# One-tile ring slots: weight and attention tiles merged into 8 KB tiles, and a ring of 23 slots instead of 21

## The chip, the cores and the metric

The kernel runs on one core of a Trainium2 chip. The core has five engines that run side by side, each with its own order of instructions: TensorE (PE; its weight loads are shown as PEld), VectorE (DVE), ScalarE (ACT), GpSimd (POOL) and SyncE (SP). Data come from the chip's large memory by DMA; here every transfer is issued by SP, in order, and carried by 16 DMA engines. The metric is the time of one execution on the device, in microseconds (us).

## What is computed

The reference is a pair of transformer blocks on 256 tokens of width 1024, in float32, followed by a norm. The first block has stick-breaking and latent attention, a feed-forward of width 2816 with a convolution of width 3, and a gate on an embedding per layer. The second has modulated norms, a convolution module, an attention over the selected keys, a pool mixer, an output projection, and a mixture of 32 experts of which each token takes two:

```python
def reference(x, ...):
    x = first_block(x, p, positions, ...)
    return second_block(x, c_2, mod_w_2, ...)

def second_block(x, c, ...):                       # one layer
    mod = silu(c) @ mod_w + mod_b                  # sh1, sc1, g1, sh2, sc2, g2
    h = rmsnorm(x, norm1_g) * (1 + sc1) + sh1
    a_val, a_gate, cq, ckv, qi, ki, wi, u_pool = split(h @ w_in)
    mix = concat([conv_module(a_val, a_gate),      # depthwise, width 31
                  dsa_attention(cq, ckv, qi, ki, wi),
                  pool_mixer(u_pool)]) @ w_out
    x = x + g1 * mix
    h = rmsnorm(x, norm2_g) * (1 + sc2) + sh2
    x = x + g2 * hier_moe(h, ..., w1, w3, w2)      # 32 experts, top 2
    return rmsnorm(x, final_g)
# an expert: (silu(h @ w1[e]) * (h @ w3[e])) @ w2[e], 1024 -> 512 -> 1024
```

The weights of one expert are 3 x 1024 x 512 float32, 6.3 MB, and all 32 are read: 201 MB of the 300 MB that the kernel moves.

## The kernel before

The work follows the reference in time. The first block and the first part of the second (to about 455 us) are matrix products whose float32 weights are cut into a high and a low part; each product is three matmuls (`mm3`, L265 to L269). A weight arrives as a raw tile of 8 KB per partition (pool `wr`, tag `raw`, three buffers), and `split` (L271) makes the two parts from it: `wh` by a cast on ScalarE and `wl` by a subtraction on VectorE (L283), each in a tile of 4 KB per partition.

The experts are the last stage (the loop at the end of the program). Expert e first multiplies the gathered tokens by w1 and w3 (`eu`, L1659), then by w2 (`ey`, L1686). Its weights come as six pieces of 1 MB, [128 x 2048] float32, 8 KB in each of 128 partitions; pieces 0 to 3 of an expert are w1 and w3, 4 and 5 are w2. Piece i is in slot i modulo the length of a ring of slots. The ring grows while the second block runs: `grow` (L1128) adds a slot and loads the next piece into it. The places of the slots are those of tiles that the program doesn't need any more, so that a load waits until their last reader is done. The 21 slots, in the order of the list `ring`, which is the order of the pieces:

- 0 to 3: pool `ewa` (step "ea" in ORDER); 4 and 5: two operands of the first block ("eh", "el"); 6: a raw tile ("e1");
- 7: the tiles qT and k2T of the second block's attention ("e2"); 8: lnT and v2 ("e3"); 9 and 10: two es tiles each ("e4"); of these pairs each tile holds half of a piece, in 4 KB per partition;
- 11 and 12: raw tiles; 13 and 14: pairs of wh and wl ("es"); 15 and 16: two operands; 17 and 18: pairs of wh and wl; 19 and 20: pool `ewc`, with room only after the router's work is closed.

`load_piece` (L1097) issues one transfer of 1 MB for a slot of one tile, and two of 512 KB for a pair; piece i is a DMA whose destination is named ew and the number of the piece, and for a pair with a further digit 0 or 1 (ew70 and ew71 are the halves of piece 7, ew11 is all of piece 11). The last three pieces are cut finer: 189 in two halves, 190 and 191 in eight of 256 KB (`exp_last`). In the expert loop six pieces are loaded behind each expert's `ey`. The tiles `fin` and `fg` of the final norm (L1639) take two slots of the ring near the end.

PE's order is written by hand, for the second block in the string ORDER (L50), whose steps are functions. The order on the other engines is made by a scheduler from the program's dependences; SP's too. SP issues in this order, so that a transfer that waits for its slot holds all behind it. The tiles are placed in pools, on two sides of the memory; `N_MP` is the number of tiles for weights of the modulation (r_mod) that are loaded ahead during the feed-forward (`F_ahead`), into a place on the right side that the second block's tiles take later.

Some names that the prediction uses: r_cq, r_ckv, r_qi, r_cv, r_wu, r_up and r_out are raw weight tiles of the second block; w_lt the parts of r_cq and r_ckv; gq, nrow, pw, rw and rb small operands; y_n the normed input, res_ple the first block's last summand; cb a sum of the width-31 convolution on POOL (L1255), s_a the pool mixer's running sums there (L1278 to L1288); ppt_d the transposes of the attention's weights (L778), pgs those of the gate matrix (L1655).

Of the kernel before, what the change touches and what calls it, by code (L numbers as in the profile page):

```python
# [20 lines left out]
P = 128  # L21
D = 1024
# [12 lines left out]
CONV2 = 31  # L35
N_A = 4
N_B = 3
N_C = 2
N_TAP = 12
# [5 lines left out]
OUT_G = ()  # L45
N_MP = 6
MOE_K = 2
X_AT = {(2, 9): 4, (31, 9): 1, (31, 10): 1}
LAST = 'y01 y12 x2 m02 y24 m24'
ORDER = 'qi0 kT0 qi1 kT1 ix0 ix1 cv0 li0 li1 cv1 ea ea lo0 lo1 ae lw ea ea va0 up eh el qk0 qk1 qk2 qk3 va1 d0 sm0 d1 po sm1 w3 e1 e2 c60 c61 w1 dT0 do0 c70 c71 c20 w2 dT1 c30 do1 tp e3 e4 e4 rl g1 c21 c31 c40 w0 ct e1 e1 c50 c51 c41 es es co'  # L50
W_AT = (2,)
# [13 lines left out]
def block_pair_kernel(ctx, tc, A, out, dbg=None):  # L65
# [205 lines left out]
    def split(raw, name, shape, gain=None, eng=V, first=()):  # L271
        n = math.prod(shape)
        vs = []
        for tg in ("wh", "wl"):
            v = wsp.tile([P, 1024], F32R, tag=tg, name=f"{name}_{tg}")[:, :n]
            if len(shape) == 2:
                v = v.rearrange("p (a b) -> p a b", a=shape[0])
            elif len(shape) == 3:
                v = v.rearrange("p (a b c) -> p a b c", a=shape[0], b=shape[1])
            vs.append(v)  # L280
        if gain is None:
            hi = S.copy(vs[0], raw)
            lo = eng.tensor_tensor(vs[1], raw, vs[0].bitcast(F32), op=ALU.subtract)  # L283
            for i, l in zip((hi, lo), first):
                after(i, *l)
                l[:] = [i]
        else:
            act(vs[0], raw, AF.Copy, scale=gain)
            V.scalar_tensor_tensor(vs[1], raw, gain, vs[0].bitcast(F32), op0=ALU.mult, op1=ALU.subtract)
        return vs  # L290
# [351 lines left out]
    def mla_weights():  # L642
        wqv = raw_pk("w_q_up", 0, (2, 768), "r_wqup")
        wqn, wqr = [[wsp.tile([P, 1024], F32R, tag=t_, name=f"{nm}_{t_}")[:, :2 * n].rearrange("p (k n) -> p k n", k=2)
                     for t_ in ("wh", "wl")] for nm, n in (("wqn", 512), ("wqr", 256))]
        for k in range(2):
            src = wqv[:, k, :].rearrange("p (h d) -> p h d", d=96)
            hv, lv = [t[:, k, :].rearrange("p (h d) -> p h d", d=64) for t in wqn]
            S.copy(hv, src[:, :, 0:64])
            V.tensor_sub(lv, src[:, :, 0:64], hv.bitcast(F32))  # L650
            for r in range(2):
                s3 = src[:, r::2, 64:96]
                hv, lv = [t[:, k, :].rearrange("p (c r d) -> p c r d", r=2, d=ROPE)[:, :, 1 - r, :] for t in wqr]
# [441 lines left out]
    etiles, ring, last = {}, [], []  # L1095

    def load_piece(i):  # L1097

        e, kind = divmod(i, 6)
        p_, tag, shape = ring[i % len(ring)]  # L1100
        if i >= 6 * N_EXP - 2:

            assert tag == "ew"
            v = p_.tile(shape, F32, tag=tag, name=f"ew{i}").rearrange("p (j k n) -> p j k n", j=4, k=2)
            last.append((v, kind - 4))
# [5 lines left out]
            return  # L1111
        if isinstance(tag, tuple):
            ts = [p_.tile([P, 1024], F32, tag=tg, name=f"ew{i}{k}") for k, tg in enumerate(tag)]
            for k, t_ in enumerate(ts):
                load(t_, packed("exp", i, 1024, 1024 * k))
        else:
            t_ = p_.tile(shape, F32, tag=tag, name=f"ew{i}")
            if len(shape) == 3:
                t_ = t_.rearrange("p k n -> p (k n)")
            ts = [t_[:, 1024 * k:1024 * k + 1024] for k in range(2)]  # L1120
            if i < 6 * N_EXP - 3:
                load(t_, packed("exp", i, 2048))
            else:
                for k in range(2):
                    load(ts[k], packed("exp", i, 1024, 1024 * k))
        form = "p (m n) -> p m n" if kind < 4 else "p (j n) -> p j n"
# [11 lines left out]
    bp = pool("b2", 1, mt, side="right")  # L1138
    esp = pool("b2e", 4, mt, side="right")
    m2 = pool("m2", 1, mt, side="right")  # L1140
    def tmp2(name):
        return esp.tile([P, D], F32, tag="es", name=name)

# [5 lines left out]

    lnT = bp.tile([P, 4, SEQ], F32, tag="lnT", name="lnT")[:, 0:3]  # L1150
    wi = bp.tile([P, NB, 8], F32, name="wi")
    qiT = bp.tile([P, 4, SEQ], F32, tag="qT", name="qiT")
    kiT = bp.tile([P, SEQ], F32, tag="ki", name="kiT")
# [22 lines left out]
    def ln_in(b):  # L1176
# [3 lines left out]
        if not lns:  # L1180
            lns[-1] = tmp2("ln2").rearrange("p (b n) -> p b n", b=2)
        ln = lns[b] = lns[-1][:, b, 0:384]
# [123 lines left out]

    k2T = bp.tile([P, 4, SEQ], F32, tag="k2T", name="k2T")
    v2 = halves(bp.tile([P, D], F32, tag="v2", name="v2"))
    lw, q2 = [], []

    def lat_load():
        q2.append(bp.tile([P, 4, SEQ], F32, tag="qT", name="q2T"))
        wu = raw_pk("w_lat2", 0, (4, 512), "r_wu")
        lw.extend(wu[:, 2 * i:2 * i + 2] for i in range(2))
# [19 lines left out]
    def dsa_softmax(b):  # L1334
        es2[b] = es_tiles(b, f"es2{b}", tmp2)
        softmax(lg2[b], b, 64.0 ** -0.5, selb[b], es2[b], f"d{b}")

    def dsa_T(b):
        pts2[b] = [tmp2(f"PT2{b}{kb}").rearrange("p (h q) -> p h q", h=8) for kb in range(b + 1)]
        att_T(es2[b], b, pts2[b], f"d{b}")  # L1340
# [57 lines left out]
    def router_load():  # L1398
# [9 lines left out]
             "ae": lambda: act_set("exp_and_others", SET_LATE[1]),  # L1408
             "e1": lambda: grow(wr, 1, "raw"), "es": lambda: grow(wsp, 1, ("wh", "wl")),
             "e2": lambda: grow(bp, 1, ("qT", "k2T")), "e3": lambda: grow(bp, 1, ("lnT", "v2")),  # L1410
             "e4": lambda: grow(esp, 1, ("es", "es")), "g1": lambda: M2.update(g1=mod_bc2("g1", 1, 0))}
    for i in range(4):
# [142 lines left out]
    grow(ap_, 1, "al", (P, KC, SEQ))  # L1555
    grow(wsp, 2, ("wh", "wl"))
    grow(ewc, N_C)

# [49 lines left out]
    for e in range(N_EXP):  # L1608
# [261 lines left out]
```

## Time and profile before

| | |
|---|---|
| median of 3 runs | 966.21 us (964.25 to 966.93) |
| the profiled execution | 965.9 us, its span 964.1 us |
| PE busy | 796.6 us (83%) |
| DVE, ACT, POOL busy | 450.4 (47%), 322.1 (33%), 96.3 us (10%) |
| moved by DMA | 301.24 MB, 312 GB/s over the span |

The profile is of one execution. The span runs from the first to the last instruction that it shows, and 1.8 us of the execution's time lie around it. Busy shares are means over stages with different limits, so that the stages are read apart, by windows of the time axis. "Idle before" is the time that an engine stood still ahead of a group of instructions, with what ended most of it. The queue of SP shows when a transfer was issued and what its issue waited for.

### The profile page before, as it was taken

How to read it: one execution, taken by the hardware profiler on the slowest of the kernel's cores; microseconds unless marked ns; L12 is line 12 of the kernel's file. 1: busy time of each engine (PE TensorE's matmuls, PEld its weight loads, DVE VectorE, ACT ScalarE, POOL GpSimd, SP SyncE). 2: the span in 40 equal slices, each digit the busy share in tenths (PEclk: the TensorE clock that was granted, in tenths of full speed). 3: DMA queues.
4: the chain of work that ended last, by engine and by line, in shares of the span. 5: the costliest groups of instructions: out<-in, count | busy, mean ns of one | idle time of the engine just before them, and what ended most of it. 6: DMA issues, size and time to landing. Idle time of an engine off the chain costs nothing. (4 is left out here: it accounts for less than half of the span.)

```text
span 964.1 us, 17534 instructions
## 1 busy us (share of the span) xinstructions
PE 796.6 (83%) x7228; PEld 571.5 (59%) x7228; DVE 450.4 (47%) x992; ACT 322.1 (33%) x635; POOL 96.3 (10%) x178
## 2 busy tenths in 40 slices
PE   5999989999999996996988987676677676756874
PEld 5978759999999873984675644233343242422422
DVE  5656667766766767589863322112121121211213
ACT  5637755555555665456741000000000000000100
POOL 1321310000000115107010000000000000000000
PEclk9999999999999998898898999879797897897978
DMA  7857788865454545855289999999999999999994
GB/s 267 274 220 271 267 343 317 306 217 177 171 193 162 188 161 162 329 223 197 80 340 372 413 421 415 418 418 416 421 414 422 414 422 415 419 416 418 418 414 168
DMA packets 55975, 301.24 MB, mean 312 GB/s; under 512 B 6480, under 2 KB 7508, under 8 KB 30292
## 3 DMA queue, kind: packets, MB, share of 16 engines
q1 hardware_dynamic: 55892, 300.08, 79.7%
q8 instruction: 58, 0.95, 0.4%
q14 instruction: 25, 0.20, 0.1%
HBM read 299.01 MB, written 1.05 MB: 311 GB/s over the span
## 5 line engine op out<-in xcount | busy, mean ns | idle before, releaser
L1659 PE MATMUL eu<-ew,XT 128*32 128x256 f32 x2048 | 144.9, 409 | 58.5 <-DMA ew<-in_exp_dram 58.2
L1659 PEld LDWEIGHTS eu<-ew,XT 128*32 128x32 f32 x2048 | 58.9, 114 | 134.3 <-DMA ew<-in_exp_dram 74.9
L77 ACT ACTIVATE hm<-eu 128x128 f32<-128x128 f32 x32 | 8.9, 277 | 340.5 <-PE eu L1659 340.5
L1686 PE MATMUL ey<-ew,hmT 128*32 128x256 f32 (+2 forms) x1088 | 85.0, 449 | 33.5 <-DMA ew<-in_exp_dram 22.5
L1672 DVE TENSOR_TENSOR hm<-hm,eu 128x128 f32<-128x128 f32 x32 | 9.2, 287 | 153.2 <-ACT hm L77 153.2
L1686 PEld LDWEIGHTS ey<-ew,hmT 128*32 128x32 f32 x1088 | 33.2, 125 | 73.0 <-DMA ew<-in_exp_dram 35.1
L1697 DVE TENSOR_TENSOR eys<-ey,g2y 128x256 f32<-128x256 f32 x31 | 13.2, 425 | 108.3 <-PE ey L1686 108.3
L269 PE MATMUL u<-hF_h,w_g_wl 128*128 128x256 f32 x168 | 47.6, 283 | 0.0
L267 PE MATMUL u<-hF_h,w_g_wh 128*128 128x256 f32 x168 | 47.5, 283 | 0.0
L268 PE MATMUL u<-hF_l,w_g_wh 128*128 128x256 f32 x168 | 47.5, 283 | 0.0
L216 POOL TENSOR_SCALAR ep_fin<-msf 128x2 f32<-128x2 f32 x1 | 0.2, 236 | 456.8 <-DVE msf L1776 456.8
L268 PE MATMUL u<-hF_l,w_v_wh 128*128 128x256 f32 x160 | 45.3, 283 | 0.0
L269 PE MATMUL u<-hF_h,w_v_wl 128*128 128x256 f32 x160 | 45.3, 283 | 0.0
L267 PE MATMUL u<-hF_h,w_v_wh 128*128 128x256 f32 x160 | 45.2, 283 | 0.0
L1588 PE MATMUL moe<-eys,gT 32*128 32x256 f32 (+1 forms) x528 | 41.8, 430 | 1.4 <-DVE eys L1710 1.4
L1622 PEld LDWEIGHTS px<-hr,x 128*128 128x128 f32 x256 | 35.1, 223 | 5.5 <-issue 2.4
L283 DVE TENSOR_TENSOR w_dn_wl<-r_d,w_dn_wh 128x1024 fp32r<-128x1024 f32 x22 | 27.0, 1225 | 24.4 <-ACT w_dn_wh L77 24.4
L77 ACT ACTIVATE XT<-px,c_SH,c_G 128x128 f32<-128x128 f32 x32 | 14.6, 457 | 69.8 <-DVE XT L1630 69.8
L1669 DVE COPY gT<-pgs 128x256 f32<-128x256 f32 x32 | 13.6, 424 | 51.6 <-PE pgs L1655 51.4
L1622 PE MATMUL px<-hr,x 128*128 128x128 f32 x256 | 36.9, 310 | 0.7 <-DVE hr L1614 0.7
L283 DVE TENSOR_TENSOR w_v_wl<-r_gv,w_v_wh 128x1024 fp32r<-128x1024 f32 x22 | 30.2, 1372 | 12.0 <-ACT w_v_wh L77 12.0
L269 PE MATMUL dn<-w_dn_wh,acl 128*128 128x512 f32 x88 | 34.5, 393 | 0.1
(568 smaller groups left out, 1961.2 us busy)
## 6 DMA issues: line engine op xcount, KB each, us to landing
ew<-in_exp_dram SPq DMA_DIRECT2D x117, 1024.0 KB, 15.3
ew<-in_exp_dram SPq DMA_DIRECT2D x146, 512.0 KB, 12.6
r_mod<-in_mod_w_dram SPq DMA_DIRECT2D x24, 1024.0 KB, 7.8
r_gv<-in_w_up_dram SPq DMA_DIRECT2D x22, 1024.0 KB, 4.9
r_d<-in_w_down_dram SPq DMA_DIRECT2D x11, 1024.0 KB, 4.9
r_wo<-in_w_o_dram SPq DMA_DIRECT2D x4, 1024.0 KB
r_pg<-in_w_ple_gate_dram SPq DMA_DIRECT2D x4, 1024.0 KB, 4.8
r_out<-in_w_out_dram SPq DMA_DIRECT2D x4, 1024.0 KB
```

Source lines behind the costliest of these rows:

```text
L77: i = getattr(nc.scalar, name)(*a, **kw)
L267: T.matmul(o, l[0], r[0], start=start, stop=False, skip_group_check=True)
L268: T.matmul(o, l[0], r[1], start=False, stop=False, skip_group_check=True)
L269: T.matmul(o, l[1], r[0], start=False, stop=stop, skip_group_check=True)
L283: lo = eng.tensor_tensor(vs[1], raw, vs[0].bitcast(F32), op=ALU.subtract)
L1588: T.matmul(moe[c][:, b * 256:b * 256 + 256][:, js], gT[rs, TB[b]], yt[rs, js], start=(start and b == 0), stop=stop, skip_group_check=True)
L1622: T.matmul(pt[:, j * P:(j + 1) * P], x[b][:, k * P:(k + 1) * P], hr[:, b], start=(b == 0), stop=(b == 1))
L1659: T.matmul(u[32 * g_:32 * g_ + 32, 0:2 * P], XT[:, k, 32 * i:32 * i + 32], etiles[6 * e + k // 2][k % 2][:, :, P * g_:P * g_ + P], start=( ...
L1669: V.tensor_copy(gT, pg[:, :SEQ])
L1672: V.tensor_mul(hm, hm, u[:, P:2 * P])
L1686: T.matmul(y[32 * c:32 * c + 32, 0:64 * (js.stop - js.start)], hmT[:, 32 * k:32 * k + 32], w2e[k].rearrange("p j (c i) -> p c j i", c=4)[: ...
L1697: V.tensor_mul(yt, y[:, 0:256], g2y)
```

## The change

The pairs of 4 KB tiles become single tiles of 8 KB: `split` makes one tile `w` whose halves are the high and the low part; lnT and v2 are the halves of `lv`, qiT (later q2T, in its place) and k2T those of `qk`; four es tiles become two double ones. Each slot of the ring is then one tile, and each piece but the last three is one transfer. The ring gets two slots more, one in `ewa` and one in `ewc`, and two more r_mod tiles are loaded ahead in the feed-forward. The scratch for DMA descriptors, 16 KB per partition by default, is set to 1 KB; this gives the room.

```diff
@@ -33 +33 @@
-N_A = 4
+N_A = 5
 N_B = 3
-N_C = 2
+N_C = 3
...
-N_MP = 6
+N_MP = 8
...
-ORDER = 'qi0 kT0 qi1 kT1 ix0 ix1 cv0 li0 li1 cv1 ea ea lo0 lo1 ae lw ea ea va0 up eh el qk0 qk1 qk2 qk3 va1 d0 sm0 d1 po sm1 w3 e1 e2 c60 c61 w1 dT0 do0 c70 c71 c20 w2 dT1 c30 do1 tp e3 e4 e4 rl g1 c21 c31 c40 w0 ct e1 e1 c50 c51 c41 es es co'
+ORDER = 'qi0 kT0 qi1 kT1 ix0 ix1 cv0 li0 li1 cv1 ea ea lo0 lo1 ae lw ea ea ea va0 up eh el qk0 qk1 qk2 qk3 va1 d0 sm0 d1 po sm1 w3 e1 e2 c60 c61 w1 dT0 do0 c70 c71 c20 w2 dT1 c30 do1 tp e3 e4 e4 rl g1 c21 c31 c40 w0 ct e1 e1 c50 c51 c41 es es co'
@@ -140 +140 @@
+    def halves2(t):
+        return [t[:, D * i:D * i + D] for i in range(2)]
@@ -271 +274 @@ split
-        for tg in ("wh", "wl"):
-            v = wsp.tile([P, 1024], F32R, tag=tg, name=f"{name}_{tg}")[:, :n]
+        t_ = wsp.tile([P, 2048], F32R, tag="w", name=f"{name}_w")
+        for i in range(2):
+            v = t_[:, 1024 * i:1024 * i + n]
@@ -1094 +1099 @@ load_piece
+    def piece_tile(i):
+        p_, tag, shape = ring[i % len(ring)]
+        t_ = p_.tile(shape, F32, tag=tag, name=f"ew{i}")
+        return t_.rearrange("p k n -> p (k n)") if len(shape) == 3 else t_
...
-        if isinstance(tag, tuple):
-            ts = [p_.tile([P, 1024], F32, tag=tg, name=f"ew{i}{k}") for k, tg in enumerate(tag)]
-            for k, t_ in enumerate(ts):
-                load(t_, packed("exp", i, 1024, 1024 * k))
+        t_ = piece_tile(i)
+        ts = [t_[:, 1024 * k:1024 * k + 1024] for k in range(2)]
+        if i < 6 * N_EXP - 3:
+            load(t_, packed("exp", i, 2048))
         else:
...
@@ -1136 +1137 @@
-    esp = pool("b2e", 4, mt, side="right")
+    esp = pool("b2e", 2, mt, side="right")
...
+    es_t = [halves2(esp.tile([P, 2 * D], F32, tag="es", name=f"es2{i}")) for i in range(2)]
...
-    lnT = bp.tile([P, 4, SEQ], F32, tag="lnT", name="lnT")[:, 0:3]
+    lv, qk_ = [halves2(bp.tile([P, 2 * D], F32, tag=nm, name=nm)) for nm in ("lv", "qk")]
+    lnT = lv[0].rearrange("p (c t) -> p c t", c=4)[:, 0:3]
...
-    qiT = bp.tile([P, 4, SEQ], F32, tag="qT", name="qiT")
+    qiT, k2T = [t.rearrange("p (c t) -> p c t", c=4) for t in qk_]
@@ -1304 +1305 @@
-    k2T = bp.tile([P, 4, SEQ], F32, tag="k2T", name="k2T")
-    v2 = halves(bp.tile([P, D], F32, tag="v2", name="v2"))
-    lw, q2 = [], []
+    v2 = halves(lv[1])
+    lw, q2 = [], [qiT]
@@ -1332 +1331 @@
-        es2[b] = es_tiles(b, f"es2{b}", tmp2)
+        es2[b] = [t.rearrange("p (h k) -> p h k", h=8 // (b + 1)) for t in ([es_t[0][1]], es_t[1])[b]]
...
-        pts2[b] = [tmp2(f"PT2{b}{kb}").rearrange("p (h q) -> p h q", h=8) for kb in range(b + 1)]
+        pts2[b] = [t.rearrange("p (h q) -> p h q", h=8) for t in ([es_t[0][0]], es_t[0])[b]]
@@ -1406 +1405 @@ steps
-             "e1": lambda: grow(wr, 1, "raw"), "es": lambda: grow(wsp, 1, ("wh", "wl")),
-             "e2": lambda: grow(bp, 1, ("qT", "k2T")), "e3": lambda: grow(bp, 1, ("lnT", "v2")),
-             "e4": lambda: grow(esp, 1, ("es", "es")), "g1": lambda: M2.update(g1=mod_bc2("g1", 1, 0))}
+             "e1": lambda: grow(wr, 1, "raw"), "es": lambda: grow(wsp, 1, "w"),
+             "e2": lambda: grow(bp, 1, "qk"), "e3": lambda: grow(bp, 1, "lv"),
+             "e4": lambda: grow(esp, 1, "es"), "g1": lambda: M2.update(g1=mod_bc2("g1", 1, 0))}
@@ -1553 +1552 @@
-    grow(wsp, 2, ("wh", "wl"))
+    grow(wsp, 2, "w")
     grow(ewc, N_C)
@@ -1637 +1636 @@
-            fin = ap_.tile([P, KC, SEQ], F32, tag="ah", name="fin").rearrange("p (b k) t -> p b (k t)", b=2)
-            fg = ap_.tile([P, KC, SEQ], F32, tag="al", name="fg").rearrange("p k t -> p (k t)")[:, 0:D]
+            fin = bp.tile([P, 2 * D], F32, tag="lv", name="fin").rearrange("p (b n) -> p b n", b=2)
+            fg = bp.tile([P, 2 * D], F32, tag="qk", name="fg")[:, 0:D]
@@ -1856 +1855 @@
-    nc = _bacc.Bacc("TRN2", target_bir_lowering=False, num_devices=1)
+    nc = _bacc.Bacc("TRN2", target_bir_lowering=False, num_devices=1, dynamic_dma_scratch_size=1024)
```

SP has 477 instructions before and 405 after. Three places of its order follow; the number behind an underscore only tells buffers apart. The first is the transfers between the first block's end and the second conv weight r_cv1, before:

```order
L139 DMA r_qi1_4341<-in_w_in2_c_dram 128x2048
L139 DMA pw_4264<-in_pool_w_dram 128x128
L139 DMA r_cv0_4524<-in_w_in2_c_dram 128x2048
L139 DMA ew0_4677<-in_exp_dram 128x2048
L139 DMA ew1_4679<-in_exp_dram 128x2048
L139 DMA ew2_4695<-in_exp_dram 128x2048
L139 DMA r_cv1_4616<-in_w_in2_c_dram 128x2048
L139 DMA ew3_4697<-in_exp_dram 128x2048
L139 DMA ew4_4779<-in_exp_dram 128x2048
```

and now:

```order
L139 DMA r_cv0_4413<-in_w_in2_c_dram 128x2048
L139 DMA gq2_4153<-in_q_norm_g_2_dram 128x256
L139 DMA gq2_4153<-in_kv_norm_g_2_dram 128x128
L139 DMA nrow2_4126<-in_norm2_g_2_dram 32x512 x2
L139 DMA ew5_4662<-in_exp_dram 128x2048
L139 DMA ew0_4561<-in_exp_dram 128x2048
L139 DMA pw_4159<-in_pool_w_dram 128x128
L139 DMA ew1_4563<-in_exp_dram 128x2048
L139 DMA ew2_4578<-in_exp_dram 128x2048
L139 DMA ew3_4580<-in_exp_dram 128x2048
L139 DMA ew4_4582<-in_exp_dram 128x2048
L139 DMA r_cv1_4502<-in_w_in2_c_dram 128x2048
```

The conv weights r_cv0 stand ahead of gq2 and nrow2, piece 5 and pieces 0 to 4 (with pw among them) are all ahead of r_cv1; before it was pieces 0 to 2.

The second is the queue around the attention's end, from the last raw weight of the output projection r_out0 on, before (ew70 and the like are half pieces):

```order
L139 DMA r_out0_5184<-in_w_out_2_dram 128x2048
L139 DMA ew70_4923<-in_exp_dram 128x1024
L139 DMA ew71_4924<-in_exp_dram 128x1024
L139 DMA ew90_5146<-in_exp_dram 128x1024
L139 DMA ew91_5147<-in_exp_dram 128x1024
L139 DMA ew81_5143<-in_exp_dram 128x1024
L139 DMA ew100_5150<-in_exp_dram 128x1024
L139 DMA ew101_5151<-in_exp_dram 128x1024
L139 DMA ew11_5221<-in_exp_dram 128x2048
L139 DMA ew12_5223<-in_exp_dram 128x2048
```

and now, with whole pieces, in which ew8 lies in `qk`, ew9 in `lv`, ew10 and ew11 in the es tiles, ew12 and ew13 in raw tiles:

```order
L139 DMA r_out0_5047<-in_w_out_2_dram 128x2048
L139 DMA ew8_4801<-in_exp_dram 128x2048
L139 DMA ew10_5013<-in_exp_dram 128x2048
L139 DMA ew12_5082<-in_exp_dram 128x2048
L139 DMA ew9_5011<-in_exp_dram 128x2048
L139 DMA ew11_5015<-in_exp_dram 128x2048
L139 DMA ew13_5084<-in_exp_dram 128x2048
L139 DMA ew14_5104<-in_exp_dram 128x2048
```

At the place where ew90 and ew91 stood there is ew10, the double tile of the second query block's weights; ew9 comes behind ew12.

The third is the last new slots and the first slots that are used again, before (the ring has 21 slots, ew21 is the first that takes the place of an expert piece):

```order
L139 DMA ew180_5500<-in_exp_dram 128x1024
L139 DMA ew181_5501<-in_exp_dram 128x1024
L139 DMA ew19_5504<-in_exp_dram 128x2048
L139 DMA ew20_5506<-in_exp_dram 128x2048
L139 DMA ew21_5619<-in_exp_dram 128x2048
L139 DMA ew22_5621<-in_exp_dram 128x2048
L139 DMA ew23_5623<-in_exp_dram 128x2048
```

and now (23 slots, the first that takes such a place is ew23):

```order
L139 DMA ew17_5351<-in_exp_dram 128x2048
L139 DMA ew18_5353<-in_exp_dram 128x2048
L139 DMA ew19_5355<-in_exp_dram 128x2048
L139 DMA ew20_5357<-in_exp_dram 128x2048
L139 DMA ew21_5359<-in_exp_dram 128x2048
L139 DMA ew22_5361<-in_exp_dram 128x2048
L139 DMA ew23_5474<-in_exp_dram 128x2048
L139 DMA ew24_5476<-in_exp_dram 128x2048
```

The first reuse moved by two pieces.

## Rows read from the trace of the kernel before

**Rows 1.** The page, GB/s moved in 40 equal slices of the span
```profile
GB/s 267 274 220 271 267 343 317 306 217 177 171 193 162 188 161 162 329 223 197 80 340 372 413 421 415 418 418 416 421 414 422 414 422 415 419 416 418 418 414 168
```

**Rows 2.** Windows: us, engines busy (instructions), PE clock, DMA share, GB/s; expert stage
```profile
600.00:700.00 100.00, 69.03 (x792) 31.83 (x792) 16.19 (x52) 3.49 (x10) 0.00 (x0) 0.85 1.02 418
...
800.00:900.00 100.00, 71.15 (x808) 34.93 (x812) 17.79 (x56) 5.32 (x14) 0.00 (x0) 0.85 1.02 418
```

**Rows 3.** The page's groups: busy us, mean ns, idle before and its releaser
```profile
L1659 PE MATMUL eu<-ew,XT 128*32 128x256 f32 x2048 | 144.9, 409 | 58.5 <-DMA ew<-in_exp_dram 58.2
...
L269 PE MATMUL u<-hF_h,w_g_wl 128*128 128x256 f32 x168 | 47.6, 283 | 0.0
```

**Rows 4.** Waits of SP's queue: waited for, us in total, times, longest
```profile
SPq L139 <- DMA ew<-in_exp_dram: 327.2, 229, 2.7
...
SPq L139 <- PE ppt_d L778: 26.5, 1, 26.5
...
SPq L139 <- PE pgs L1655: 13.7, 7, 10.9
```

**Rows 5.** Windows between the second block's attention and expert 0
```profile
395.00:446.00 51.00, 48.96 (x388) 45.19 (x386) 41.85 (x100) 32.16 (x63) 14.13 (x22) 1.00 0.61 234
...
455.00:475.00 20.00, 17.42 (x81) 11.88 (x78) 18.16 (x52) 15.86 (x44) 0.83 (x1) 0.79 0.02 5
...
475.00:513.00 38.00, 34.82 (x240) 29.36 (x242) 25.02 (x87) 17.68 (x38) 3.53 (x8) 0.91 0.89 338
...
502.00:513.00 11.00, 8.06 (x64) 7.21 (x67) 5.86 (x36) 3.64 (x9) 0.00 (x0) 0.69 1.00 408
...
513.00:514.00 1.00, 1.00 (x18) 0.36 (x10) 1.00 (x5) 0.46 (x1) 0.00 (x0) 1.00 0.45 188
...
516.00:517.00 1.00, 0.83 (x16) 0.26 (x8) 0.11 (x1) 0.10 (x1) 0.00 (x0) 1.00 1.00 393
```

**Rows 6.** Timeline of SP's queue: start, us, issue, count
```profile
473.65 0.33 SPq L139 DMA_DIRECT2D ew<-in_exp_dram  x1
...
513.79 6.79 SPq L139 DMA_DIRECT2D ew<-in_exp_dram  x6
...
934.95 11.16 SPq L139 DMA_DIRECT2D ew<-in_exp_last_dram  x8
```

**Rows 7.** Timeline of PE, idle before in brackets: the pool product, expert 0
```profile
453.97 1.97 PE L1296 MATMUL ppl<-s_a,pw 64*64 64x256 f32 x8 [7.79 <-POOL s_a L1288]
...
512.66 1.07 PE L1659 MATMUL eu<-ew,XT 128*32 128x256 f32 x16
```

**Rows 8.** DMA view, packets of four windows: 621:638, 730:743, 535:543, 642:649
```profile
DMA packets 997, 7.25 MB, mean 426 GB/s; under 512 B 112, under 2 KB 112, under 8 KB 112
...
DMA packets 762, 5.56 MB, mean 428 GB/s; under 512 B 83, under 2 KB 83, under 8 KB 83
...
DMA packets 892, 3.27 MB, mean 409 GB/s; under 512 B 97, under 2 KB 97, under 8 KB 891
...
DMA packets 781, 2.86 MB, mean 408 GB/s; under 512 B 88, under 2 KB 88, under 8 KB 776
```

**Rows 9.** The page's queue and its issues: count, KB each, us to landing
```profile
q1 hardware_dynamic: 55892, 300.08, 79.7%
...
ew<-in_exp_dram SPq DMA_DIRECT2D x117, 1024.0 KB, 15.3
ew<-in_exp_dram SPq DMA_DIRECT2D x146, 512.0 KB, 12.6
```

**Rows 10.** Timeline of POOL: one addition cb
```profile
451.79 0.72 POOL L1255 TENSOR_TENSOR cb<-cb,pr 128x256 f32<-128x256 f32 x1
```

**Rows 11.** Timelines of DVE and SP; instructions on r_cv, first and last start
```profile
384.57 0.68 DVE L1052 TENSOR_TENSOR y_n<-y_n,SH 128x512 f32<-128x512 f32 x1
...
386.37 1.88 DVE L283 TENSOR_TENSOR w_lt_wl<-r_ckv,w_lt_wh 128x800 fp32r<-128x800 f32 x2
...
400.52 0.33 SPq L139 DMA_DIRECT2D r_cv<-in_w_in_c_dram  x1
...
L77 ACT CAST w_cv_wh<-r_cv x4: 1045/1047/1047, 403.3 to 412.0; 128x1024 fp32r<-128x1024 f32 x4
```

More of the change, by code (lines that the diff above doesn't have):

```diff
@@ L643, in mla_weights @@
         wqv = raw_pk("w_q_up", 0, (2, 768), "r_wqup")
-        wqn, wqr = [[wsp.tile([P, 1024], F32R, tag=t_, name=f"{nm}_{t_}")[:, :2 * n].rearrange("p (k n) -> p k n", k=2)
-                     for t_ in ("wh", "wl")] for nm, n in (("wqn", 512), ("wqr", 256))]
+        wqn, wqr = [[t_[:, 1024 * i:1024 * i + 2 * n].rearrange("p (k n) -> p k n", k=2) for i in range(2)]
+                    for t_, n in ((wsp.tile([P, 2048], F32R, tag="w", name="wqn"), 512),
+                                  (wsp.tile([P, 2048], F32R, tag="w", name="wqr"), 256))]
         for k in range(2):
@@ L1095, in block_pair_kernel @@
     etiles, ring, last = {}, [], []
+    def piece_tile(i):
+        p_, tag, shape = ring[i % len(ring)]
+        t_ = p_.tile(shape, F32, tag=tag, name=f"ew{i}")
+        return t_.rearrange("p k n -> p (k n)") if len(shape) == 3 else t_
     def load_piece(i):
         e, kind = divmod(i, 6)
-        p_, tag, shape = ring[i % len(ring)]
         if i >= 6 * N_EXP - 2:
-            assert tag == "ew"
-            v = p_.tile(shape, F32, tag=tag, name=f"ew{i}").rearrange("p (j k n) -> p j k n", j=4, k=2)
+            v = piece_tile(i).rearrange("p (j k n) -> p j k n", j=4, k=2)
             last.append((v, kind - 4))
@@ L1111, in load_piece @@
             return
-        if isinstance(tag, tuple):
-            ts = [p_.tile([P, 1024], F32, tag=tg, name=f"ew{i}{k}") for k, tg in enumerate(tag)]
-            for k, t_ in enumerate(ts):
-                load(t_, packed("exp", i, 1024, 1024 * k))
-        else:
[L1117 to L1125, printed above, removed]
+        t_ = piece_tile(i)
+        ts = [t_[:, 1024 * k:1024 * k + 1024] for k in range(2)]
+        if i < 6 * N_EXP - 3:
+            load(t_, packed("exp", i, 2048))
+        else:
+            for k in range(2):
+                load(ts[k], packed("exp", i, 1024, 1024 * k))
         form = "p (m n) -> p m n" if kind < 4 else "p (j n) -> p j n"
@@ L1138, in block_pair_kernel @@
     bp = pool("b2", 1, mt, side="right")
-    esp = pool("b2e", 4, mt, side="right")
+    esp = pool("b2e", 2, mt, side="right")
     m2 = pool("m2", 1, mt, side="right")
-    def tmp2(name):
-        return esp.tile([P, D], F32, tag="es", name=name)
+    es_t = [halves2(esp.tile([P, 2 * D], F32, tag="es", name=f"es2{i}")) for i in range(2)]
     def w1k(name):
@@ L1180, in ln_in @@
         if not lns:
-            lns[-1] = tmp2("ln2").rearrange("p (b n) -> p b n", b=2)
+            lns[-1] = es_t[0][0].rearrange("p (b n) -> p b n", b=2)
         ln = lns[b] = lns[-1][:, b, 0:384]
@@ L1304, in pool_out @@
                 V.scalar_tensor_tensor(lo, src, g_, hi.bitcast(F32), op0=ALU.mult, op1=ALU.subtract)
-    k2T = bp.tile([P, 4, SEQ], F32, tag="k2T", name="k2T")
-    v2 = halves(bp.tile([P, D], F32, tag="v2", name="v2"))
-    lw, q2 = [], []
+    v2 = halves(lv[1])
+    lw, q2 = [], [qiT]
     def lat_load():
-        q2.append(bp.tile([P, 4, SEQ], F32, tag="qT", name="q2T"))
         wu = raw_pk("w_lat2", 0, (4, 512), "r_wu")
```

## The prediction

> **What bounds the kernel now.** I read the profile from the end backwards, asking in each stretch which resource never stops. The row of moved bytes over 40 slices [rows 1] shows two halves: up to slice 20 the rate swings between 80 and 343 GB/s, from slice 23 on it stands at 413 to 422 until the last slice. The second half is the 32 experts, whose weights are 192 pieces of 1 MB (1.0486 MB). The stretches of 100 us there [rows 2] give 418 GB/s with a DMA share of 1.02, while TensorE is busy 69 to 71 us of 100: DMA is full, TensorE is not. The same is seen from TensorE's side: before the expert matmuls at L1659 it idles 58.5 us, of which 58.2 us end with the landing of an expert tile [rows 3]. And from the queue's side: SP, which issues every transfer in order, waits 327.2 us in 229 waits for one of its own earlier expert transfers to land [rows 4], so it always has the next one ready. From about 516 us on, the time is therefore bytes divided by rate, until the stream ends; from its last issue, which ends at 946.1 [rows 6], 18 us follow to the span's end (last landing, last expert, final norm, output).
>
> Before that, DMA is not the bound. Between 455 and 475 us it moves 5 GB/s [rows 5]: the head of SP's queue waits 26.5 us for the transposes ppt_d [rows 4], because the next free ring slot is an attention tile, and goes on at 473.65 [rows 6]. From 475 to 513 us it moves 338 GB/s on average, in the last part, 502 to 513, 408; then it runs dry: 188 from 513 to 514 and 393 again from 516 on [rows 5]. The reason is that all 21 slots of the ring are full. Expert 0's first matmuls run at 512.66 [rows 7], its first slot is reused at 513.79 [rows 6] after a wait of 10.9 us for TensorE, and the flow is back about 2.4 us later, at 516.2.
>
> So two quantities set the end: how many pieces are still to be moved when the flow resumes at 516.2, and at what rate they move.
>
> **The change part by part.**
>
> *Row length.* Eight of the 21 slots are made of two 4 KB tiles, and each piece that goes there is two transfers of 512 KB with 4 KB rows; the others are one transfer of 1 MB with 8 KB rows (146 and 117 of them [rows 9]). The stretches in which one kind alone flows can be told by their packets under 8 KB, and they differ [rows 8]: 426 and 428 GB/s where 112 of 997 and 83 of 762 packets are under 8 KB (the bookkeeping ones), 409 and 408 where 891 of 892 and 776 of 781 are. A piece takes 1048.6/427 = 2.456 us in the one form and 1048.6/408.5 = 2.567 in the other, 0.111 us more. Of the pieces 21 to 188, which is eight turns of the ring, 8 x 8 = 64 are of the slow form, and the change makes them fast: 64 x 0.111 = 7.1 us. Bounds: nothing, if it is not the row length that makes these stretches slow but something of the slots; and by the difference of the extreme rows (428 against 408, 0.120 us a piece) 7.7 us. I take 7.0.
>
> The Trainium skill, "DMA: Bandwidth & Descriptors", section "Specifications", has transfers at line rate from 512 bytes on; by that 4 KB and 8 KB rows would be equal and this term 0. The same page, "Why small descriptors are slow", charges each packet about 3 cycles; with the 850 MHz of its section "Where 436 GB/s comes from" that is an estimated 3.5 ns, and with 16 more packets per DMA engine and piece 0.056 us, so 3.6 us for 64 pieces. The rows here show 0.111 us, twice that, and the measurement decides.
>
> *Two more slots.* The ring has 23 slots: one more of pool ewa, filled during the second block's attention, and one more of ewc, filled after the router. The first reuse is now of piece 23 and not 21, by the same event: the first matmuls of expert 0. In SP's order the pieces before it are all there; if they have landed by 516.2, 169 pieces remain instead of 171: 2 x 2.456 = 4.9 us. Do they fit? Before 473 the old order has issued 8.5 pieces, the new one 9 (0 to 8), so 14 remain instead of 12.5. The freeing events behind 473.65 are those of before, with ew10 (the double tile whose transposes are waited for), ew12, ew9 and ew11 at the head. The half piece more falls into the holes that 338 GB/s against 427 leaves in the 38 us from 475 [rows 5]: 38 x 89 = 3.4 MB, three pieces. The whole piece more is the new ewc tile, which is free only at about 502; from there on DMA was full until 513.6, so it ends at 513.6 + 2.5, less some 0.3 for rows of 8 KB: 515.8, just before 516.2. Bounds: 0 if the filling is late by five microseconds or the slots come free in another order, and 5.0. I take 4.9.
>
> *Front.* Any shift of expert 0's start shifts the end one for one, as the stream resumes with it. Two r_mod transfers move into the feed-forward part, where DMA moves 161 to 217 GB/s (slices 9 to 16 [rows 1]) and TensorE waits for nothing (0.0 us before 168 of its products [rows 3]); r_cq, r_ckv, r_qi and r_cv0 move up with them. The lo parts of w_lt1 (386.37, 1.88 us for two [rows 11]) now stand on VectorE ahead of res_ple instead of behind hZ_l, and those of w_lt0 before both res_ple: between -1.5 and +1.9 us on a chain at which TensorE idles. On POOL eleven instead of ten additions cb stand before the last s_a; one takes 0.72 [rows 10], and TensorE waits 7.79 us for that s_a [rows 7], so +0.7 to +0.9. In the feed-forward the merged weight tiles change ScalarE's order, under the same cover. Sum taken: 0, bounds -2 and +3. The final tiles fin and fg move to slots whose last pieces (170 and 169) belong to expert 28, done when they are written: 0. The smaller descriptor scratch only makes room: every transfer is on SP's hardware queue [rows 9], and the expert stage would show it if not.
>
> *Sum.* -7.0 - 4.9 + 0 = -11.9 us on the profiled execution's 965.9 us (span 964.1 and 1.8 around it), 954.0; that execution is 0.3 below the median of 966.21, so about 954.3 against the median. I forecast 954.5.
>
> **Rivals.**
> - *Rows don't matter.* The slow stretches belong to the slots or to the source addresses, and a whole piece takes its 2.5 us in these slots as well. Then only the two slots count: 965.9 - 5.0 = 961. Against it: four stretches at four places of the ring split cleanly by row length [rows 8]. The 512-byte rule of the Trainium skill, "DMA: Bandwidth & Descriptors", would come out here.
> - *Depth is worth little.* The 14 pieces don't land by 516.2, because one slot is held (lv, for instance, merges lnT, dead early, with v2, which do1 reads at the end, and waits for the later of both) and, the queue being in order, holds all behind it. Then the extra pieces are moved after 516 like before: 965.9 - 7.0 = 959. For it: half tiles at the head of the old queue became whole ones. Against it: the old queue stood there just as long, at 473.65.
> - *The front comes late, slower.* r_cv1, the second half of the conv weights, now stands behind ew1 to ew4 on SP. It was issued at 400.52, and its casts end the row that runs from 403.3 to 412.0 [rows 11], so it has some 6 us to spare. If ew4's slot comes free late, then r_cv1, r_wu, r_up and r_out3 behind it are late, and TensorE, busy 48.96 of the 51 us from 395 [rows 5], stands still. This decides when expert 0 starts after 512.66 + 11.9 = 524.6: with r_cv1 issued at 425, 24.5 - 6 = 18.5 us late, the time is 965.9 - 11.9 + 18.5 = 972.5. Against it: by the addresses of the tiles, what lies in those places before (mod tiles, SH1) is read for the last time by the y_n sum that ends at 385.25 [rows 11], 15 us before r_cv1's turn, and five whole pieces take 12.3 us.
> - *TensorE becomes the bound*: no, 71 of 100 us [rows 2] leaves 29 where a gain of 12 us in 430 takes 3 of 100.
>
> **How the numbers follow.** Forecast (both terms, within 4 us) 0.66; rows don't matter 0.11; depth is worth little 0.11; late front 0.06; both terms gone, or one and a front late by a few microseconds, 0.06. A measurement of this kernel tells some 0.3%, 2.9 us, from no change. Faster takes the first three, 0.88; same 0.06; slower 0.06. The forecast's own range is 950.5 to 958; to leave out no more than 2 in 10 it reaches to the first two rivals: 949.5 to 962.
>
> **What would show it.** Rows: the expert stretches at 425 to 428 GB/s instead of 418, in all five turns, and no issue of 512 KB but piece 189's. Depth: DMA doesn't run dry between 513 and 516, the 23rd piece has landed by 516.5, and SP's wait for pgs stands before ew23. Front: expert 0's first matmul at 512.7, within 2 us. The last expert issue, done at 946.1 before [rows 6], should be done near 934. I am wrong if the rate stays at 418, if DMA still runs dry near 515, or if expert 0 starts past 516.

## The result and the profile after

The changed kernel takes 954.84 us (median of 4 runs, 952.62 to 956.68) against 966.37 (4 runs, 964.25 to 966.93): the ratio is 0.9884, with a 95% interval of 0.9854 to 0.9913. The forecast was 954.5. Its profiled execution took 953.5 us, with a span of 951.4.

The moved bytes in 40 slices, from the page of the changed kernel:

```profile
GB/s 270 265 217 291 248 325 351 341 236 197 174 211 187 177 133 168 328 186 177 71 332 423 424 419 425 420 423 422 422 424 421 425 422 423 423 421 425 421 422 175
```

The full rate begins at slice 22, one earlier than before [rows 1], and stands a little higher, at 419 to 425. The windows of the changed kernel (columns as in [rows 2]) show where the flow begins and what it is:

```profile
475.00:513.00 38.00, 34.83 (x252) 28.77 (x252) 25.88 (x92) 17.66 (x39) 3.54 (x8) 0.91 0.91 366
...
502.00:513.00 11.00, 8.60 (x72) 7.09 (x76) 6.47 (x33) 3.75 (x8) 0.00 (x0) 0.69 1.01 424
513.00:514.00 1.00, 1.00 (x24) 0.61 (x20) 1.00 (x6) 0.00 (x0) 0.00 (x0) 1.00 1.02 410
514.00:515.00 1.00, 0.87 (x17) 0.26 (x8) 0.15 (x1) 0.07 (x1) 0.00 (x0) 1.00 1.01 426
...
600.00:700.00 100.00, 66.74 (x800) 31.95 (x797) 15.86 (x51) 3.78 (x11) 0.00 (x0) 0.88 1.01 422
...
800.00:900.00 100.00, 73.15 (x849) 36.85 (x845) 18.43 (x58) 6.80 (x19) 0.00 (x0) 0.85 1.01 423
```

Against [rows 5], 475 to 513 us carry 366 GB/s and not 338, and the dry moment at 513 is gone: 410 and 426. Against [rows 2], 422 and 423 stand where 418 was, with TensorE busy for 67 to 73 us of 100, so that DMA is still the bound. SP's waits and issues:

```profile
SPq L139 <- DMA ew<-in_exp_dram: 339.7, 163, 3.7
...
SPq L139 <- PE ppt_d L783: 23.0, 1, 23.0
SPq L139 <- PE pgs L1654: 12.6, 7, 10.1
```

```profile
511.83 5.92 SPq L139 DMA_DIRECT2D ew<-in_exp_dram  x5
...
918.68 14.98 SPq L139 DMA_DIRECT2D ew<-in_exp_last_dram  x8
946.14 2.32 SPq L139 DMA_DIRECT2D out_dram<-fin  x4
```

The queue still stops for ppt_d and for pgs, a little shorter than in [rows 4] (23.0 against 26.5 us, 12.6 against 13.7), and goes on behind ppt_d at 472.39 (473.65 before, [rows 6]). In this profile the second stop no longer empties the DMA engines. The last expert issue is done at 933.66 and not at 946.11 [rows 6], 12.4 us earlier; the span is 12.7 us shorter. Expert 0 started on TensorE at 510.70, 2 us earlier than in [rows 7]; the second execution of this kernel below, where it is 0.4 us later, shows that one profile can't settle this:

```profile
510.70 1.07 PE L1658 MATMUL eu<-ew,XT 128*32 128x256 f32 x16
```

### The profile page after: what moved, and what is told of

Same layout as the page of the kernel before. It is cut to its first block, busy times and chain, and to the rows that moved or that the text cites. A ratio compares the mean times of both kernels' runs of the same rounds, so it can differ in the third digit from the quotient of the medians.

```text
span 951.4 us, 17340 instructions
## 1 busy us (share of the span) xinstructions
PE 789.6 (83%) x7228; PEld 570.8 (60%) x7228; DVE 449.6 (47%) x992; ACT 322.8 (34%) x635; POOL 115.7 (12%) x178
## 5 line engine op out<-in xcount | busy, mean ns | idle before, releaser
L1658 PE MATMUL eu<-ew,XT 128*32 128x256 f32 x2048 | 141.6, 408 | 54.2 <-DMA ew<-in_exp_dram 53.9
L1685 PE MATMUL ey<-ew,hmT 128*32 128x256 f32 (+2 forms) x1088 | 82.8, 441 | 35.1 <-DMA ew<-in_exp_dram 23.3
L959 POOL TENSOR_TENSOR ac<-cv_g,cv_v 128x256 f32<-128x256 f32 x22 | 36.4, 1657 | 153.8 <-ACT w_g_w L77 121.8
L272 PE MATMUL u<-hF_h,w_g_w 128*128 128x256 f32 x168 | 47.6, 283 | 0.0
L270 PE MATMUL u<-hF_h,w_g_w 128*128 128x256 f32 x168 | 47.5, 283 | 0.0
L271 PE MATMUL u<-hF_l,w_g_w 128*128 128x256 f32 x168 | 47.5, 283 | 0.0
L271 PE MATMUL u<-hF_l,w_v_w 128*128 128x256 f32 x160 | 45.3, 283 | 0.0
L272 PE MATMUL u<-hF_h,w_v_w 128*128 128x256 f32 x160 | 45.3, 283 | 0.0
L270 PE MATMUL u<-hF_h,w_v_w 128*128 128x256 f32 x160 | 45.2, 283 | 0.0
L270 PE MATMUL dn<-w_dn_w,ach 128*128 128x512 f32 x88 | 34.5, 392 | 0.7 <-ACT ach L77 0.7
L271 PE MATMUL dn<-w_dn_w,ach 128*128 128x512 f32 x88 | 34.6, 393 | 0.0
L272 PE MATMUL dn<-w_dn_w,acl 128*128 128x512 f32 x88 | 34.6, 393 | 0.0
L1621 PEld LDWEIGHTS px<-hr,x 128*128 128x128 f32 x256 | 31.7, 205 | 4.3 <-issue 3.3
```

Of the source, the lines that this page charges most:

```text
L270: T.matmul(o, l[0], r[0], start=start, stop=False, skip_group_check=True)
L271: T.matmul(o, l[0], r[1], start=False, stop=False, skip_group_check=True)
L272: T.matmul(o, l[1], r[0], start=False, stop=stop, skip_group_check=True)
L959: G.tensor_tensor(a_, gt, vl, op=ALU.mult)
L1621: T.matmul(pt[:, j * P:(j + 1) * P], x[b][:, k * P:(k + 1) * P], hr[:, b], start=(b == 0), stop=(b == 1))
L1658: T.matmul(u[32 * g_:32 * g_ + 32, 0:2 * P], XT[:, k, 32 * i:32 * i + 32], etiles[6 * e + k // 2][k % 2][:, :, P * g_:P * g_ + P], start=( ...
```

## The experiments

Times are medians, and ratios are to the kernel before, run on the same chip, with their 95% interval. In the windows the last three columns are again PE clock, DMA share and GB/s.

**The changed kernel again**, no edit.

> The changed kernel once more, for comparison on the same chip. Both theories: 953 to 956 us, as measured, with expert 0's first matmuls near 510.7 us and 422 GB/s in the expert stage.

Measured: 954.88 us, ratio 0.9881 (0.9863 to 0.9898). The single runs go from 953.59 to 957.46, and the profiled one was the longest. In it TensorE reaches expert 0 later:

```profile
513.09 1.07 PE L1658 MATMUL eu<-ew,XT 128*32 128x256 f32 x16
```

and DMA, which the first profile shows full across the first reuse, runs short a little behind it (516 to 517 us, 517 to 520):

```profile
516.00:517.00 1.00, 1.00 (x24) 0.51 (x16) 0.53 (x3) 0.00 (x0) 0.00 (x0) 1.00 0.82 213
517.00:520.00 3.00, 1.90 (x33) 0.95 (x29) 0.58 (x2) 0.28 (x1) 0.00 (x0) 1.00 0.93 306
```

This start is 2.4 us behind that of the first profile of the same program (510.70) and 0.4 behind [rows 7]. So the expected 510.7 was a miss, and differences of a microsecond or two in one profile's front say nothing of the change. The first profile has 418 and 423 GB/s in these two windows: whether 23 slots carry the flow across the wait for expert 0 without a gap differs between executions.

**21 slots**, with the long rows kept:

```diff
-N_A = 5
+N_A = 4
-N_C = 3
+N_C = 2
-ORDER = '... lw ea ea ea va0 ...'
+ORDER = '... lw ea ea va0 ...'
```

(fin and fg as before the change.)

> One part undone: the changed kernel with 8 KB tiles and rows, but 21 ring slots (one less in ewa, one less in ewc; fin and fg in the slots of before). Theory (the number of slots counts by the pieces left at expert 0's start): two pieces more, 2 x 2.48 us, so 5.0 us above the changed kernel, about 959.8 us, 422 GB/s, and DMA dry again for 2 to 3 us before the first reuse. Rival (depth is worth little, the gain is all in the rate): within 1 us of the changed kernel, 955.

Measured: 960.57 us, ratio 0.9945 (0.9931 to 0.9959), 5.7 us above the changed kernel. The rate is the changed kernel's, and DMA is dry again before the first reuse at 512.87:

```profile
512.00:513.00 1.00, 1.00 (x18) 0.44 (x10) 1.00 (x5) 0.46 (x1) 0.00 (x0) 1.00 0.17 66
513.00:514.00 1.00, 1.00 (x19) 0.55 (x21) 0.98 (x4) 0.46 (x1) 0.00 (x0) 1.00 0.20 57
514.00:515.00 1.00, 1.00 (x24) 0.65 (x20) 1.00 (x6) 0.00 (x0) 0.00 (x0) 1.00 0.71 180
...
600.00:700.00 100.00, 71.18 (x810) 33.35 (x806) 16.18 (x52) 3.49 (x10) 0.00 (x0) 0.82 1.01 422
```

The two slots are worth two pieces (5.7 us against 5.0 expected); that depth is worth little is refuted.

**4 KB rows everywhere**, in two transfers a piece, with 23 slots:

```diff
-        if i < 6 * N_EXP - 3:
-            load(t_, packed("exp", i, 2048))
-        else:
-            for k in range(2):
-                load(ts[k], packed("exp", i, 1024, 1024 * k))
+        for k in range(2):
+            load(ts[k], packed("exp", i, 1024, 1024 * k))
```

> The other part undone and overdone: 23 slots of 8 KB tiles, but every piece is two transfers of 512 KB with 4 KB rows. Theory A (row length, sized as the changed kernel shows it: the mean rate rose from 417.9 to 422.5 GB/s when 64 of 171 pieces became long-rowed, so 0.072 us a piece): 167 x 0.072 = 12 us above, about 967 us, 410 GB/s in the expert stage. Theory B (sized as predicted, 0.111 us a piece): 18.5 us above, about 973 us, 408 GB/s beside 427. Rival (rows don't matter, it was the slots): 955 us and 422 GB/s.

Measured: 969.49 us, ratio 1.0034 (1.0022 to 1.0046), 14.6 us above the changed kernel, between the two sizes. The rate is that of theory A, and there is a dip that neither expected, behind the four small loads fgr:

```profile
545.00:550.00 5.00, 5.00 (x60) 4.19 (x52) 1.83 (x6) 1.05 (x3) 0.00 (x0) 1.00 0.97 347
550.00:555.00 5.00, 4.57 (x74) 2.42 (x66) 2.79 (x13) 1.05 (x3) 0.00 (x0) 1.00 0.92 300
...
600.00:700.00 100.00, 73.33 (x788) 28.71 (x788) 16.05 (x52) 3.50 (x10) 0.00 (x0) 0.83 1.03 411
```

The slots are those of the changed kernel, so that they are not what makes a piece slow. Whether it is the row or the second transfer isn't told apart here; the run with two transfers of half the partitions was to do that.

**Six r_mod tiles ahead**, as before the change:

```diff
-N_MP = 8
+N_MP = 6
```

> One part undone: the changed kernel with only six r_mod tiles loaded ahead, so that the last two r_mod transfers stand behind r_pg again and r_cq, r_ckv and the lo parts of w_lt come as late as before; POOL's order of the convolution sums stays that of the changed kernel. Theory (the 2 us by which expert 0 starts earlier in the changed kernel come from the front moving up): expert 0's first matmuls at about 512.7 instead of 510.7, and 956.8 us. Rival (they come from the second block's attention, ScalarE and POOL, and not from the transfers): expert 0 at 510.7 and 955 us.

Measured: 956.18 us, ratio 0.9898 (0.9882 to 0.9914), 1.3 us above the changed kernel, with overlapping intervals; expert 0 starts at 511.67. Neither theory is borne out: since the changed kernel itself starts it at 510.70 or 513.09, there were no 2 us to explain.

**Two transfers a piece with 8 KB rows**, each of half the partitions:

```diff
-            load(t_, packed("exp", i, 2048))
+            src = packed("exp", i, 2048)
+            for k in range(2):
+                load(t_[64 * k:64 * k + 64], src[64 * k:64 * k + 64])
```

> What slows the 4 KB form, the row or the number of transfers: the changed kernel with every piece as two transfers of 512 KB again, but each of 64 partitions with 8 KB rows. Theory (row length): 422 GB/s in the expert stage, and about 2 us above the changed kernel, 957 us, for the dip near 550 us that the smaller transfers in flight cost in the run with 4 KB rows. Rival (two transfers a piece cost, whatever their rows): 411 GB/s and about 967 us, as with the 4 KB rows. Open for both: 64 partitions at a time may spread worse over the engines, which would show as a rate under 411.

Measured: 1233.29 us, with single runs from 1205.86 to 1320.14, so that the size is rough; all are over 240 us above the kernel before. In the profile (1223.55 us) the expert stage runs at 279 to 313 GB/s with a DMA share of 1.02:

```profile
600.00:700.00 100.00, 61.31 (x542) 28.09 (x542) 12.32 (x40) 2.94 (x8) 0.00 (x0) 0.62 1.02 279
...
800.00:900.00 100.00, 66.07 (x611) 30.64 (x607) 12.90 (x42) 3.21 (x9) 0.00 (x0) 0.65 1.02 313
```

By the DMA share the engines are busy all the time, and they move a quarter to a third less: the open case; why was not traced. It drowns the question, which is left to the two runs with one transfer a piece.

**24 slots, the last one late**:

```diff
-N_C = 3
+N_C = 4
...
-            XT = ek.tile([P, KC, P], F32, tag="XT", name=f"XT{e}")
+            XT = ek.tile([P, KC, P], F32, tag="XT", name=f"XT{e}", bufs=1)
...
-        if e == N_EXP - 3:
+        if e == N_EXP - 2:
```

(bufs=1 for gT, hm, hmT and eys too.)

> One slot more than the change: a third form of the ring with 24 slots (four in ewc; room from single buffers for XT, gT, hm, hmT and eys; fin and fg taken one expert later). Theory (a slot counts only if it has landed by the first reuse; in the changed kernel DMA is busy without a gap across that moment, so the 23 slots are just about filled then): nothing or little, 954 to 955 us, with no dry stretch near 514 us. Rival (each slot is worth a piece, 2.5 us): 952.4 us.

Measured: 954.13 us, ratio 0.9881 (0.9864 to 0.9898), that of the changed kernel. In its profile expert 0 starts at 510.63, as early as in the first profile of the changed kernel, and DMA flows on through the first reuse, as it did there:

```profile
513.00:514.00 1.00, 1.00 (x28) 0.57 (x23) 1.00 (x6) 0.00 (x0) 0.00 (x0) 1.00 1.00 418
514.00:515.00 1.00, 0.80 (x16) 0.23 (x8) 0.08 (x1) 0.14 (x1) 0.00 (x0) 1.00 1.09 459
```

Nothing or little is what was measured; the rival's 952.4 us, a ratio of 0.9863, lies just outside the interval. With the later start of the second profile of the changed kernel (513.09), where 23 slots left DMA short, a 24th was not seen.

**The descriptor scratch**, a pair with one order of instructions: 21 slots, six r_mod tiles, 16 KB and 1 KB. The edit to the pair's second:

```diff
-    nc = _bacc.Bacc("TRN2", target_bir_lowering=False, num_devices=1)
+    nc = _bacc.Bacc("TRN2", target_bir_lowering=False, num_devices=1, dynamic_dma_scratch_size=1024)
```

> The descriptor scratch alone, first of a pair with one order of instructions: 21 slots of 8 KB tiles, six r_mod tiles ahead, scratch of 16 KB as before the change. Theory (no transfer uses it): the same time as its twin with 1 KB, within 0.5 us; from the runs with 21 slots and with six r_mod tiles, 960.6 + 1.3 = 962 us. Rival (the smaller scratch slows or speeds the queue): a difference of more than 1.5 us, and another rate than 422 GB/s in the expert stage.

> The second of the pair: 21 slots of 8 KB tiles, six r_mod tiles ahead, scratch of 1 KB. This is the change without its two slots and without the two r_mod tiles, so it is also the row length alone. Theory: the same as its twin within 0.5 us, about 962 us; against the kernel before that is 4 to 4.7 us less, 64 slow pieces at 0.065 to 0.072 us. As predicted (0.111 us a piece): 7 us less, 959 us.

Measured: 960.92 us, ratio 0.9950 (0.9937 to 0.9964), and 960.97 us, ratio 0.9945 (0.9931 to 0.9960). The scratch does nothing for the time that these runs could tell. Both lie 1 us below the 962 that was added up from the two single runs. Both are the merged tiles alone, without the two slots and the two r_mod tiles: 4.7 us less than before.

**One transfer, 4 KB rows**, and **one transfer, 2 KB rows** (the edit of the first is shown; the second has 4 in place of each 2 that counts the rows, and 512 in place of each 1024):

```diff
-            load(t_, packed("exp", i, 2048))
+            a_ = A["exp"]
+            load(t_.rearrange("p (k n) -> p k n", k=2),
+                 bass.AP(tensor=a_.tensor, offset=a_.offset + i * P * 2048, ap=[[2048, P], [P * 2048 + 1024, 2], [1, 1024]]))
```

> Row length apart from the number of transfers: the changed kernel with every piece as one transfer of 1 MB and 128 partitions as before, but of two rows of 4 KB a partition, which lie apart in the source. For that the second half of each piece is read from the piece behind it, so this kernel computes with other weights. Theory (row length): 410 to 412 GB/s in the expert stage, 169 x 0.065 = 11 us above the changed kernel, 966 us; the rest of the 969.5 us with two transfers a piece was the dip near 550 us. Rival (the number of transfers): 422 GB/s and 955 us.

> The same with four rows of 2 KB a partition and piece, from four pieces. Theory (a fixed cost for each row: 0.065 us a piece for eight rows more in each of the 16 DMA engines, 8 ns a row): 24 rows more than with 8 KB, 0.195 us a piece, 392 GB/s, 33 us above the changed kernel, 988 us. Rival (the loss is one of 4 KB rows, as of some boundary, and not of each row): 966 us, as with 4 KB.

Measured: 965.44 us, ratio 0.9998 (0.9990 to 1.0007), and 989.92 us, ratio 1.0258 (1.0244 to 1.0271). The packets of the window from 600 to 700 us (DMA view), first of the changed kernel, then of these two:

```profile
DMA packets 5798, 42.25 MB, mean 422 GB/s; under 512 B 647, under 2 KB 647, under 8 KB 647
```

```profile
DMA packets 10656, 41.16 MB, mean 412 GB/s; under 512 B 627, under 2 KB 627, under 8 KB 10648
```

```profile
DMA packets 19581, 38.99 MB, mean 390 GB/s; under 512 B 593, under 2 KB 593, under 8 KB 19573
```

The transfers are the same in number and size; the rows alone are halved and halved again. From 422 to 412 GB/s a piece takes 2.485 and 2.545 us, 0.060 more for 8 more rows in each of 16 engines, 7.5 ns a row; to 390 it takes 2.689, 0.204 more for 24 rows, 8.5 ns. Row length it is, and a cost of some 8 ns for each row. The rows of one partition lie apart in the source in these two kernels; but the run with two transfers a piece, whose 4 KB rows lie side by side there, shows the same rate (411), so that neither the place of the rows nor the second transfer sets it. Of the 14.6 us of that run, 10.6 are the rows and 4.0 come with the second transfer, of which the dip at 545 to 555 us (412 against 347 and 300 for 5 us each) is 2.1; the rest wasn't traced.

**24 slots, the extra one early**, in ewa instead of ewc (the edit is against the run with 24 slots):

```diff
-N_A = 5
+N_A = 6
-N_C = 4
+N_C = 3
-ORDER = '... lw ea ea ea va0 ...'
+ORDER = '... lw ea ea ea ea va0 ...'
```

> The 24th slot where it can be filled early: six slots in ewa and three in ewc instead of five and four, otherwise the kernel with 24 slots. The extra piece is loaded with the others of ewa between 380 and 446 us, where DMA moves 199 GB/s. Theory (a slot counts by what has landed at the first reuse): a piece less to move afterwards, 2.5 us below the changed kernel, about 952.3 us. Rival (more than 23 slots gain nothing, TensorE or something else sets the time): 954 to 955 us, as with the late 24th slot.

Measured: 952.55 us, ratio 0.9873 (0.9856 to 0.9889). It is 2.3 us below the changed kernel and 1.6 below the late 24th slot, as the theory has it, but the intervals overlap, so that this is not shown. (The 199 GB/s of the expectation are those of 395 to 446 us in the changed kernel; from 380 on it is 235.) In its profile expert 0 starts at 512.09, and DMA still runs short behind the first reuse, at 287 and 303 GB/s from 515 to 517 us: even 24 slots do not carry every execution across.

**The same, with the raw tile's slot ahead**:

```diff
-ORDER = '... do1 tp e3 e4 e4 rl g1 c21 c31 c40 w0 ct e1 e1 c50 ...'
+ORDER = '... do1 tp rl g1 c21 c31 c40 w0 e1 e4 e3 e4 ct e1 c50 ...'
...
+            if i in (11, 12, 13):
+                after(ins, lins[10])
```

(The last two lines put pieces 11 to 13 behind piece 10 on SP.)

> The same with the raw tile's slot put ahead of the es and lv slots in the ring and on SP, so that its piece is not held behind the transposes ppt_d that SP waits for until 472 us: it can go at about 464, when the last lo part of r_out2 is made. Theory (DMA is idle there, and what lands there need not be moved after the first reuse, as long as slots are left unfilled then): 0.5 to 1.5 us below the version without it, 951 to 952 us. Rival (the ring is full by the first reuse in any case, or r_out0 comes late and holds TensorE): the same or more.

Measured: 951.36 us, ratio 0.9851 (0.9836 to 0.9866), the lowest of all. But not by the mechanism that was expected. SP's queue waits there for the lo part of r_out2 instead, until 474.93, longer than for ppt_d in the run without the new order (23.8 us):

```profile
SPq L139 <- DVE w_out_w L287: 24.8, 1, 24.8
```

```profile
474.93 0.80 SPq L139 DMA_DIRECT2D ew<-in_exp_dram  x2
```

The piece doesn't go at 464, and the 1.2 us to the version without the new order are less than the intervals tell. It beats the kernel before clearly; against the changed kernel the intervals still touch (an upper end of 0.9866 against a lower end of 0.9863).

## Why the prediction was right

**The bound.** Right: DMA is full from 502 us to the end of the stream, but for a gap of a few microseconds behind the first reuse in some executions, and the edits that changed the time clearly changed either its rate or the number of slots.

**Two more slots, -4.9 us.** Right in size and mechanism. Without them the time is 5.7 us more (960.57 against 954.88), and with six r_mod tiles in both kernels 4.8 (960.97 against 956.18). The fill is as tight as the working had it, with 0.4 us between 515.8 and 516.2: in the first profile DMA runs on without a gap, in the second it runs short from 516 to 520 us, and the late 24th slot brought nothing that the interval tells. The queue goes on behind ppt_d at 472.39 and 474.39 in the two profiles, on both sides of 473.65, as assumed.

**Row length, -7.0 us.** Right in mechanism, too large in size: the merged tiles alone bring 4.7 us (960.97 against 965.65, 3.9 to 6.7 by the interval), 0.073 us for each of the 64 pieces and not 0.111; the rates alone, 422 against 412 GB/s, give 0.060, and the 425 to 428 GB/s that were to show the term did not come. The step that failed is the reading of [rows 8]: 426 to 428 GB/s, from stretches of 13 and 17 us chosen between slow ones, was taken for the rate of 8 KB rows. Where they flow alone it is 422. The prediction had the row that tells it: 107 pieces at 427 and 64 at 408.5 make 171 x 1048.6/(107 x 2.456 + 64 x 2.567) = 420 GB/s, and [rows 2] say 418; with 422 and 412 it is 418. In the mixed stream the stretches of long rows thus ran above their own rate and those of short rows (408 and 409 against 411 and 412 alone) below; what makes them do that wasn't tried. How far a short window is off by itself can be read: cut into windows of 13 us from 560 to 900 us, the changed kernel, which has long rows only, shows 419 to 429 GB/s, and the kernel with one transfer of 4 KB rows, in windows of 8 us, 407 to 421. So a single window of [rows 8] can be off by 6 GB/s and more.

On the rule that was weighed against this: the line rate from 512 bytes on, of the Trainium skill, "DMA: Bandwidth & Descriptors", section "Specifications", is refuted here by 390, 412 and 422 GB/s at 2, 4 and 8 KB. The cost of each packet that the Trainium skill gives in "Why small descriptors are slow", on its page "DMA: Bandwidth & Descriptors", has the right form, with 8 ns measured beside the 3.5 that were estimated from it. The count in that estimate was wrong: a piece has 128 rows of 8 KB or 256 of 4 KB, which is 8 more in each of 16 engines and not 16, so that the rule gives an estimated 0.028 us a piece, half of what the prediction made of it.

**Front, 0 us.** Right within its bounds. The kernel without the two r_mod tiles is 0.4 us (960.97 against 960.57) and 1.3 us slower (956.18 against 954.88), below what the intervals tell. The first part did occur, at its upper bound: with the lo parts of w_lt1 ahead of res_ple the wait for y_n grows from 7.6 to 8.5 us (first line before, second after), and the transposes of y_n start at 383.40 and not at 381.54, 1.9 us later (383.89 in the second profile). At expert 0, which starts earlier in one profile and later in the other, nothing of it can be told. The second part isn't seen: the wait for s_a shrinks, from 7.8 to 4.2 us, and TensorE waits 2.9 us for the score operand `qk` just before:

```profile
PE pt_n L263 <- DVE y_n L1052: 7.6, 1, 7.6
...
PE pt_n L266 <- DVE y_n L1057: 8.5, 1, 8.5
PE ppl L1297 <- POOL s_a L1289: 4.2, 1, 4.2
PE sc_d L731 <- ACT qk L77: 2.9, 2, 1.9
```

The pool product that waits for s_a starts at 453.21 in this profile and at 454.74 in the second, on both sides of 453.97 [rows 7].

**The sum.** The chain of runs (before, merged tiles, two slots, two r_mod tiles) goes down by 4.7, 4.8 and 1.3 us, 10.8 in all; these are the steps of one chain, so that their sum is no check of its own, and in the other order the r_mod tiles bring 0.4 and the slots 5.7. The forecast's -11.9 had 2.3 too much on the rows and up to 1.3 too little on the front, so that part of its closeness is errors that cancel, and luck.

**The rivals.** Rows that don't matter and depth of little worth are both refuted. A late front: r_cv1 was issued at 400.24, within 0.3 us of [rows 11], with six pieces ahead of it (the prediction counted five); in the second profile at 401.77. TensorE as the bound: no, it is busy 67 to 73 us of 100. The scratch: 0.05 us between the twins.

## What to carry to other kernels

Where a stream of weights sets the end, ask two things of each edit: at what rate do the bytes flow, and how many are left when the buffers are first reused. Here a buffer that is filled before the first reuse was worth a piece, and one that comes free only just before it nothing that could be told. Merge half tiles so that rows and transfers are as long as they can be. And before a rate is taken from short chosen stretches, weigh the rates by their shares and compare with the long window that holds both.

## What was not expected of the hardware

Two transfers of 64 partitions each, with the same 8 KB rows, ran at 279 to 313 GB/s with all DMA engines busy, where one of 128 partitions runs at 422. And the same bytes in rows of 4 KB cost 4.0 us more as two transfers a piece than as one (969.49 against 965.44), half of it in one dip behind four loads of 1 KB on the same queue.
